# Neighbourhood attention: low parts of the keys padded to 128 rows, two heads together through transposes and value products, bias in one tile

## The chip, the cores and the metric

One Trainium2 chip, one of its cores. The metric is the device time of one execution in microseconds (us). TensorE (PE) multiplies, with its weight loads shown as PEld; VectorE (DVE), ScalarE (ACT) and GpSimd (POOL) do the rest, and SyncE (SP) issues most DMAs. "Line" L141 is line 141 of the kernel before.

## The reference

Two layers of a hybrid backbone over 512 latent tokens (an 8 x 64 grid) and 256 context tokens, 1024 features, all in float32. Layer 0 mixes by eight heads of two-dimensional neighbourhood attention (64 features each) beside four mLSTM heads; layer 1 by multi-head latent attention; each layer ends in a gated FFN with a depthwise convolution of width 3. The change touches the neighbourhood attention:

```python
def row_block(args):                 # one row of queries
    ...                              # bias: learned 2-D table in the 8 x 16 window, -1e30 outside
    s_lat = einsum('bqhd,bkhd->bhqk', q_row, k_band) * scale + bias
    s_ctx = einsum('bqhd,bkhd->bhqk', q_row, k_c) * scale
    p = softmax(concatenate([s_lat, s_ctx], axis=-1), axis=-1)
    nl = kh * GRID_W
    return einsum('bhqk,bkhd->bqhd', p[..., :nl], v_band) + einsum('bhqk,bkhd->bqhd', p[..., nl:], v_c)
```

A latent query thus reads its window and all context keys under one softmax. The context tokens attend to each other in the same eight heads (`dense_attention`, without a bias).

## The kernel before

The kernel is written with a tile framework: instructions are given in program order, tiles come from rings with a number of buffers, and a scheduler with its own estimate of durations then orders each engine's queue. Program order is priority; an instruction whose operands it expects late may be passed by later ones. Blocks under `tc.high_priority` (weight loads, `mix_split`) go ahead of their place. All semaphores come from the framework.

**Precision.** Most matmuls run in the one-pass float32r format. For accuracy an operand is split into `hi`, its rounded value, and `lo`, the rest, and a product is hi·hi + lo·hi + hi·lo, three matmuls into the same PSUM region (`proj`, `proj_steps`). The value products and transposes are plain float32; a float32 product leaves two records in the trace.

**Pairs of heads.** The eight heads go in four pairs, p_ = 0 to 3. `na_proj` computes queries, keys and values of a pair in 48 steps of three matmuls each: eight k tiles, 512 latent and 256 context columns, three projections (tiles `qp`, `kp`, `vp`). For head s of the pair, `qs[s]` holds the high part of the query in its own 64 rows and the low part in the other 64. `kd[s]` holds the high part of the key twice, in both halves of the rows. One 128-row matmul of `qs[s]` with `kd[s]` therefore gives hi·hi + lo·hi. The third product, hi·lo, is a 64-row matmul of the query's own half with `kl`, one tile that holds the low parts of both heads in its halves. `vtok` holds the values, tokens on the partitions: seven tiles of window columns and two of context.

**Attention of a pair** (`na_attn`). The 512 queries are four blocks j of 128 (8 rows x 16 columns), and each reads 256 latent keys (8 rows x 32 columns from column `KSTART[j]`) and 256 context keys.

- `scores(s)`, per j: four matmuls into a PSUM tile `sp`, kd and kl for the 256 latent columns, then kd and kl for the 256 context columns. One DVE instruction (L816) adds the bias, writes `P[j]` and takes the maximum; ACT takes the exponential, POOL divides by the sum. Then `fill(nf[0])` lets some projection steps of the next pair follow.
- `weighted(s, P)`: for each quarter `ks` of the 512 keys, four transposes into `ptp`, a copy to `pT` (ACT and DVE in turn), and products with `vtok` into `ops_`, 64 output rows per head: one of 512 columns for a context quarter, four of 128 for a latent one.
- `scores_c(s)`, `weighted_c(s, ...)`: the same for the context's own queries (`spc`, `Pc`, `ptc`, `pTc`, `opc`).

The order in a pair is scores of head 0, scores of head 1, `weighted` 0, `scores_c` 0, `weighted` 1, the output copy to `mix`, `scores_c` 1, `weighted_c` 0 and 1. `NF = (2, 3, 4, 6)` says how many projection steps follow a score block, a quarter's transposes, a context score and a context transpose; the last pair has `NF3 = (0, 1, 2, 3)` and, instead of a projection, 14 steps of the output projection (tile `yps`). The first pair is projected within the mLSTM stage.

**Bias.** Per head a DMA (L801) brings three kinds of 128 x 256 (left, inner, right blocks) from HBM into `bias_t[s]`, one of two tiles of 3 x 512 whose second halves are zero and belong to the context keys. The DMAs go through SP's queue, as do the weight loads (`wload`, L180).

**Elsewhere.** `ps_w` hands out three one-bank PSUM tiles in turn. `scratch` and the tag `sq` are small rings of `sqp`, two tiles each. `fcw` holds the FFN's convolution weights of both layers, loaded at the start. The gate rows of the mLSTM (`gps`, L581) are float32 products with weight tiles of 128 rows x 32 columns, k tile k in column group k mod 4 of the array.

Of the kernel before, what the change touches and what calls it, by code (L numbers as in the profile page):

```python
# [9 lines left out]
F32 = mybir.dt.float32  # L10
# [56 lines left out]
def hybrid_backbone_kernel(ctx: ExitStack, tc: tile.TileContext, *aps):  # L67
# [14 lines left out]
    def psum_open(**n):  # L82
        """n: tiles per tag; A tiles hold two banks, the others one"""
        if psum:
            psum["st"].close()
        st = ExitStack()
        psum["st"], psum["n"], psum["split"] = st, n, False
        psum["p"] = st.enter_context(tc.tile_pool(name="ps" + "".join(f"{k}{v}" for k, v in n.items()), bufs=1,
                                                  space=bass.MemoryType.PSUM, reuse_waits="tile"))
# [41 lines left out]
    fcw = cload("ffn_conv", [128, 2, 2 * NH, 4])  # L131
# [26 lines left out]
    def table(func, after):  # L158
        """has the activation table loaded ahead of its first use"""
        t = tiny.tile([128, 8], F32, tag="rv", name="tab")  # L160
        act(t[:, 0:1], after, func)
# [21 lines left out]
    def proj(o, w, x, cols, ks=tuple(range(KD)), first=True, last=True):  # L183
        """out[m, cols] = sum over k tiles of W[k, m]^T x[k, cols]; w units hold [k][128]."""
# [60 lines left out]
    def ada(l, part, get, pool, bufs):  # L245
        """modulation part (1024 columns) of layer l; column group j of the array takes 256 of them"""
# [19 lines left out]
    def ada_q(l, part, q, get, pool, bufs):  # L266
        """256 columns of a part; column group j of the array takes a quarter of the k tiles"""
# [59 lines left out]
    def mod_scale(l, part, norm, name, nv=2):  # L327
        """norm_g * (1 + scale)"""
# [14 lines left out]
    class Seg:  # L343
        """a run of tokens: width, offset in the padded layout, offset in the packed one, modulation column"""
# [30 lines left out]
    def step(n):  # L375
        """n steps of the norm chains in flight, oldest first"""
# [7 lines left out]
    def until(sg):  # L384
        """finish the chain of a run of tokens"""
# [3 lines left out]
    def sums4(ps, w, srcs, first, last):  # L389
        """column sums of four tiles, side by side in the array"""  # L390
# [4 lines left out]
    def sums_bc(ps, sg, name):  # L395
        """rstd on all partitions from the sums of sums4"""
# [7 lines left out]
    class YNorm:  # L404
        """sum of squares over the feature tiles of a branch output, then the gated residual"""
# [68 lines left out]
    # =============================== layer 0 ===============================  # L474
# [4 lines left out]
    with ExitStack() as l0:  # L479
# [38 lines left out]
        def x0_scale(q):  # L518
            """x * rstd * A for a quarter of the feature tiles"""
# [16 lines left out]
        def token_major(which, wus):  # L536
            """W[k, 512] with tokens on the output partitions; a k tile per step"""
# [39 lines left out]
        # gate rows, four feature tiles side by side in the array; the shift comes in with the bias  # L577
# [58 lines left out]
        # tri[:, 0]: k <= m ; tri[:, 1]: k >= m ; tri[:, 2]: row 127 ; tri[:, 3]: row 0  # L636
# [12 lines left out]
        # additive masks: msk[:, 0] allows column <= row, msk[:, 1] allows column >= row  # L649
# [9 lines left out]
        # running maxima of e along the scan, chunks and heads on partitions (the directions 32 apart)  # L659
# [52 lines left out]
        # -M in three exact pieces (rows 0, 32, 64 on), for its sums over the partitions to be rows of it  # L712
# [30 lines left out]
        def na_proj(p_, nq, res):  # L743
            """queries, keys and values of a pair of heads, in steps"""
# [19 lines left out]
            kl = nq.tile([128, T], F32R, tag="kl", name="kl")  # L764
            for s in range(2):
                r0, r1 = (0, 64) if s == 0 else (64, 128)
                act(kd[s][r0:r1, :], kp_[r0:r1, 0:T])
                tt(V, kl[r0:r1, :], kp_[r0:r1, 0:T], fr(kd[s][r0:r1, :]), ALU.subtract)
# [22 lines left out]
        def na_attn(p_, nw, bias_t, fill, qs, kd, kl, vtok):  # L791
# [6 lines left out]
            def scores(s):  # L798
                hd = 2 * p_ + s
                r0, r1 = rows[s]  # L800
                nc.sync.dma_start(out=bias_t[s][:, :, 0:256], in_=a["na_bias"][hd].rearrange("k p n -> p k n"))  # L801
# [5 lines left out]
                for j in range(4):  # L807
                    sp = ps_w("sp")
                    q_ = qs[s][:, j * 128:(j + 1) * 128]
                    qh_ = qs[s][r0:r1, j * 128:(j + 1) * 128]  # L810
                    lat = sp[:, 0:256].rearrange("p (f r c) -> p f r c", f=2, r=8)
                    mm(lat, q_, klat(kd[s], j), True, False)
                    mm(lat, qh_, klat(kl[r0:r1], j), False, True)
                    mm(sp[:, 256:512], q_, kd[s][:, TX:T], True, False)
                    mm(sp[:, 256:512], qh_, kl[r0:r1, TX:T], False, True)
                    V.tensor_tensor_reduce(out=P[j], in0=sp, in1=bias_t[s][:, BKIND[j], :],  # L816
# [9 lines left out]
            def weighted(s, P):  # L826
                r0, r1 = rows[s]
                for ks in (2, 3, 0, 1):
# [4 lines left out]
                    pT = nw.tile([128, 512], F32, tag="pT", name="pT", bufs=2)  # L833
                    if ks % 2:
# [3 lines left out]
                    if ks >= 2:  # L838
                        mm(ops_[r0:r1, 0:TX], vtok[:, 7 + ks - 2, r0:r1], pT, ks == 2, False)
                    else:  # L840
                        for j in range(4):
                            vi = VTILE[KSTART[j] + 16 * ks]
                            mm(ops_[r0:r1, j * 128:(j + 1) * 128], vtok[:, vi, r0:r1],
                               pT[:, j * 128:(j + 1) * 128], False, ks == 1 and j == 3)

            def scores_c(s):
                r0, r1 = rows[s]
                sp = ps_w("spc")
                for j in range(2):
                    q_ = qs[s][:, TX + j * 128:TX + (j + 1) * 128]  # L850
                    qh_ = qs[s][r0:r1, TX + j * 128:TX + (j + 1) * 128]
                    mm(sp[:, j * 256:(j + 1) * 256], q_, kd[s][:, TX:T], True, False)
                    mm(sp[:, j * 256:(j + 1) * 256], qh_, kl[r0:r1, TX:T], False, True)
# [5 lines left out]
                Pc = nw.tile([128, 512], F32, tag="P", name="Pc", bufs=8)  # L859
# [9 lines left out]
            def weighted_c(s, Pc, opc):  # L869
                r0, r1 = rows[s]  # L870
# [6 lines left out]
                pT = nw.tile([128, 512], F32, tag="pT", name="pTc", bufs=2)  # L877
                V.tensor_copy(out=pT, in_=pt)
                for kt in range(2):
                    mm(opc[r0:r1, 0:TC], vtok[:, 7 + kt, r0:r1], pT[:, kt * 256:(kt + 1) * 256],  # L880
                       kt == 0, kt == 1)
# [7 lines left out]
            weighted(0, P0)  # L889
            c0 = scores_c(0)  # L890
            weighted(1, P1)
            act(mix[:, p_, 0:TX].rearrange("p (r j c) -> p j r c", j=4, r=8),
                ops_.rearrange("p (j r c) -> p j r c", j=4, r=8))
            c1 = scores_c(1)
            opc = ps_x("opc")
            weighted_c(0, c0, opc)
            weighted_c(1, c1, opc)
            act(mix[:, p_, TX:T], opc[:, 0:TC])

# [1 line left out]
        if True:  # L901
# [4 lines left out]
            def ml_in(hd):  # L906
                qk = []
                for w_ in range(2):
# [9 lines left out]
                    # 2 silu(u) = (tanh(u / 2) + 1) u  # L918
# [16 lines left out]
            def ml_decay(hd, sT):  # L935
                """decay matrices times scores, both directions"""
                ws = []
                for d in range(2):
                    pump(MP[0][d])
                    # w^T[s, t]; fwd admits s <= t  # L940
# [108 lines left out]
        with ExitStack() as nas:  # L1049
# [3 lines left out]
            bias_t = [nb_.tile([128, 3, 512], F32, name=f"bias{i}") for i in range(2)]  # L1053
            for t_ in bias_t:
                act(t_[:, :, 256:512], zpad[:, 0, 0:1].unsqueeze(2).to_broadcast([128, 3, 256]))
# [10 lines left out]
            def wo_steps():  # L1066
                """the first output tiles but for the last pair of heads"""
# [28 lines left out]
        mix_split(3)  # L1096
# [592 lines left out]
```

## Time and profile before

| what | value |
|---|---|
| runs shown | 1888.87, 1886.98, 1885.5 us; median 1886.98 us |
| the profiled execution, first to last instruction (its only own time on record) | 1887.4 us |
| mean granted TensorE clock | 0.984 |
| PE busy | 97% of the span, 10546 matmul records |
| DVE, ACT, POOL busy | 62%, 40%, 14% |
| the stage of neighbourhood attention, 291.1 to 502.8 us | 211.7 us, PE busy 208.87 us |

Rows of the order of time read: start in us, length in us, engine, line, operation, output<-inputs, weight tile (rows*columns) and output form, number merged. Rows of groups read: line, engine, operation, output<-inputs, form, count | busy us, mean ns of one | idle time of the engine ahead of them and what ended it. Rows of waits read: the engine and what waited <- what it waited for: us in total, times, longest us. The ends of matmuls are modelled and neighbours overlap, so what a matmul costs is seen from one start to the next.

### The profile page before, as it was taken

Reading aid. Unit: us, or ns where it says so; the run is one execution under the profiler, and the core shown is the slowest. Engines: PE = TensorE matmul, PEld = TensorE weight load, DVE = VectorE, ACT = ScalarE, POOL = GpSimd, SP = SyncE. Lnnn points to the kernel's source line nnn. Section 1 sums busy time; section 2 is a strip of 40 time slices with the busy share of each in tenths; the row PEclk is TensorE's granted clock in tenths of the full one; section 3 lists DMA queues with packets and bytes.
Section 4 is the critical chain, followed back from the end, with each engine's and each line's share of the span. In section 5 each row is a group of like instructions: output and inputs, shape, how many; then the busy total and the mean of one; then the engine's idle time right before and its main releaser. Section 6 shows DMA issues by size and latency. Waiting matters only on the chain. (4 is left out here: it accounts for less than half of the span.)

```text
span 1887.4 us, 26712 instructions
## 1 busy us (share of the span) xinstructions
PE 1825.2 (97%) x10546; PEld 1492.1 (79%) x10546; DVE 1173.2 (62%) x2230; ACT 748.0 (40%) x1295; POOL 258.8 (14%) x312
## 2 busy tenths in 40 slices
PE   7999999999999999999999999899998999999997
PEld 4777787776678888888888887778887888888885
DVE  3383676345537676767666456888885574556655
ACT  3333454343334432222221334567784444334232
POOL 1000132122222000000000002444451100000000
PEclk8999999999999999999999999999999999999998
DMA  8343431112310333434432210100011213333221
GB/s 300 107 134 112 135 101 48 48 51 78 117 40 28 107 123 112 124 111 145 134 112 78 79 57 24 41 12 13 12 34 56 68 58 99 101 94 118 89 90 45
DMA packets 63196, 162.26 MB, mean 86 GB/s; under 512 B 6256, under 2 KB 19744, under 8 KB 63072
## 3 DMA queue, kind: packets, MB, share of 16 engines
q1 hardware_dynamic: 61616, 156.52, 26.4%
q0 software_dynamic: 1312, 3.91, 0.6%
q8 instruction: 83, 1.36, 0.3%
q14 instruction: 41, 0.34, 0.1%
q10 hardware_dynamic: 144, 0.13, 0.0%
HBM read 158.44 MB, written 2.10 MB: 85 GB/s over the span
## 5 line engine op out<-in xcount | busy, mean ns | idle before, releaser
L147 ACT ACTIVATE whi<-wraw 128x1024 fp32r<-128x1024 f32 x186 | 195.5, 1059 | 466.3 <-PE pu L141 220.0
L150 DVE TENSOR_TENSOR wlo<-wraw,whi 128x1024 fp32r<-128x1024 f32 x183 | 222.9, 1224 | 223.6 <-ACT whi L147 218.0
L141 PE MATMUL pu<-h,whi 128*128 128x258 f32 (+1 forms) x1280 | 318.6, 339 | 0.0
L141 PEld LDWEIGHTS pu<-h,whi 128*128 128x128 f32 x1280 | 219.7, 189 | 28.6 <-issue 0.8
L141 PE MATMUL pd<-hid,whi 128*128 128x512 f32 (+1 forms) x864 | 233.3, 358 | 1.5 <-DVE acc L150 1.5
L141 PE MATMUL pu<-h,wlo 128*128 128x512 f32 (+1 forms) x640 | 216.8, 339 | 0.0
L141 PEld LDWEIGHTS pd<-hid,whi 128*128 128x128 f32 x864 | 152.3, 188 | 28.4 <-DVE acc L150 3.1
L150 POOL TENSOR_TENSOR ry<-rv,mhalf 128x2 f32<-128x2 f32 (+2 forms) x26 | 23.8, 915 | 1013.9 <-DVE rv L153 1011.9
L141 PE MATMUL pd<-hid,wlo 128*128 128x512 f32 (+1 forms) x432 | 153.1, 356 | 0.0
L156 DVE SCALAR_TENSOR_TENSOR u<-pu,c_ffn_conv,u 128x769 f32<-128x769 f32 (+1 forms) x156 | 138.0, 885 | 21.6 <-ACT u L147 19.7
L150 DVE TENSOR_TENSOR acc<-pd,acc 128x512 f32<-128x512 f32 (+1 forms) x192 | 109.2, 586 | 48.6 <-PE pd L141 47.3
L141 PEld LDWEIGHTS pu<-h,wlo 128*128 128x128 f32 x640 | 121.0, 189 | 13.6
L141 PE MATMUL pu<-lb,whi 128*128 128x512 f32 x304 | 119.7, 394 | 0.0
L141 PE MATMUL pu<-hb,whi 128*128 128x512 f32 x304 | 119.0, 391 | 0.0
L141 PE MATMUL pu<-hb,wlo 128*128 128x512 f32 x304 | 118.3, 389 | 0.0
L156 DVE SCALAR_TENSOR_TENSOR av<-aw,s,av 128x512 f32<-128x512 f32 x140 | 102.4, 749 | 20.4 <-DMA aw<-in_ada_w_dram 19.9
L153 POOL TENSOR_SCALAR P<-P,rl 128x768 f32<-128x768 f32 (+1 forms) x96 | 85.6, 893 | 148.3 <-DVE nm L153 60.5
L141 PEld LDWEIGHTS pd<-hid,wlo 128*128 128x128 f32 x432 | 81.2, 189 | 11.7
L147 ACT ACTIVATE u<-pu,c_ffn_conv 128x770 f32<-128x770 f32 (+1 forms) x78 | 68.4, 877 | 39.5 <-PE pu L141 39.4
L141 PE MATMUL sp<-kr,qh 128*128 128x512 f32 (+1 forms) x256 | 72.6, 359 | 4.3 <-DVE kr L150 3.3
L141 PE MATMUL yps<-h,whi 128*128 128x512 f32 (+1 forms) x256 | 69.6, 360 | 0.0
L141 PEld LDWEIGHTS pu<-hb,whi 128*128 128x128 f32 x304 | 57.1, 188 | 13.2
(442 smaller groups left out, 3861.6 us busy)
## 6 DMA issues: line engine op xcount, KB each, us to landing
wraw<-in_ffn_up_dram SPq DMA_DIRECT2D x88, 512.0 KB, 3.6
aw<-in_ada_w_dram SPq DMA_DIRECT2D x112, 256.0 KB, 2.7
wraw<-in_ffn_down_dram SPq DMA_DIRECT2D x44, 512.0 KB, 3.6
aw<-in_ada_w_dram SPq DMA_DIRECT2D x40, 512.0 KB, 4.7
wraw<-in_w_in_dram SPq DMA_DIRECT2D x20, 512.0 KB, 3.6
wraw<-in_w_tok_dram SPq DMA_DIRECT2D x8, 512.0 KB, 4.2
wraw<-in_w_out_dram SPq DMA_DIRECT2D x8, 512.0 KB, 3.5
wraw<-in_w_o_dram SPq DMA_DIRECT2D x8, 512.0 KB, 3.5
```

The lines of the kernel that those rows point to most:

```text
L141: PE.matmul(out=o, lhsT=l, rhs=r, start=start, stop=stop)
L147: S.activation(out=o, in_=i, func=func, **kw)
L150: e.tensor_tensor(out=o, in0=x, in1=y, op=op)
L153: e.tensor_scalar(out=o, in0=x, scalar1=s1, scalar2=s2, op0=op0, op1=op1)
L156: V.scalar_tensor_tensor(out=o, in0=x, scalar=s, in1=y, op0=op0, op1=op1)
```

## The change

The low parts of the keys get a tile for each head, with zeros in the other head's rows, filled once for each of the two buffers (`kl_pair`); every score matmul then takes the whole `qs[s]`. Transposes and copies of a quarter are done for both heads (`turned`), and its products, the two heads in turn, follow one quarter later (`products`). The context's products alternate in the same way. `pT` has four buffers, the context probabilities move to the ring `sq`, and the bias of both heads lies in one tile of seven slices, three for each head and one of zeros. The convolution weights of layer 1 are loaded ahead of its FFN.

```diff
-    fcw = cload("ffn_conv", [128, 2, 2 * NH, 4])
+    fcw = [cload("ffn_conv", [128, 2 * NH, 4], a["ffn_conv"][:, 0])]
...
+        klz = {}
+        def kl_pair(nq):
+            if nq not in klz:
+                klz[nq] = [nq.tile([128, T], F32R, name=f"kl{s}") for s in range(2)]
+                for s in range(2):
+                    o = slice(64, 128) if s == 0 else slice(0, 64)
+                    ts(G, klz[nq][s][o, :], zpad[o, 0, 0:1].to_broadcast([64, T]), 1.0, 0.0, ALU.mult, ALU.add)
+            return klz[nq]
...
-            kl = nq.tile([128, T], F32R, tag="kl", name="kl")
+            kl = kl_pair(nq)
...
-                tt(V, kl[r0:r1, :], kp_[r0:r1, 0:T], fr(kd[s][r0:r1, :]), ALU.subtract)
+                tt(V, kl[s][r0:r1, :], kp_[r0:r1, 0:T], fr(kd[s][r0:r1, :]), ALU.subtract)
...
-                nc.sync.dma_start(out=bias_t[s][:, :, 0:256], in_=a["na_bias"][hd].rearrange("k p n -> p k n"))
+                nc.sync.dma_start(out=bias_t[:, 3 * s:3 * s + 3, :], in_=a["na_bias"][hd].rearrange("k p n -> p k n"))
...
-                    mm(lat, qh_, klat(kl[r0:r1], j), False, True)
+                    mm(lat, q_, klat(kl[s], j), False, True)
...
-                    mm(sp[:, 256:512], qh_, kl[r0:r1, TX:T], False, True)
-                    V.tensor_tensor_reduce(out=P[j], in0=sp, in1=bias_t[s][:, BKIND[j], :],
+                    mm(sp[:, 256:512], q_, kl[s][:, TX:T], False, True)
+                    bi = 3 * s + BKIND[j]
+                    V.tensor_tensor_reduce(out=P[j].rearrange("p (a b) -> p a b", a=2),
+                                           in0=sp.rearrange("p (a b) -> p a b", a=2), in1=bias_t[:, bi:7:6 - bi, :],
...
-            def weighted(s, P):
...
+            def turned(ks, Ps):
+                pts = []
+                for s, P in enumerate(Ps):
                     pt = ps_w("ptp")
                     for j in range(4):
                         tr(pt[:, j * 128:(j + 1) * 128], P[j][:, ks * 128:(ks + 1) * 128])
                     fill(nf[1])
+                    pT = nw.tile([128, 512], F32, tag="pT", name="pT", bufs=4)
+                    if s:
                         V.tensor_copy(out=pT, in_=pt)
                     else:
                         act(pT, pt)
+                    pts.append(pT)
+                return pts
+            def products(ks, pts):
+                if ks >= 2:
+                    for s, (r0, r1) in enumerate(rows):
+                        mm(ops_[r0:r1, 0:TX], vtok[:, 7 + ks - 2, r0:r1], pts[s], ks == 2, False)
+                    return
+                for j in range(4):
+                    vi = VTILE[KSTART[j] + 16 * ks]
+                    for s, (r0, r1) in enumerate(rows):
+                        mm(ops_[r0:r1, j * 128:(j + 1) * 128], vtok[:, vi, r0:r1],
+                           pts[s][:, j * 128:(j + 1) * 128], False, ks == 1 and j == 3)
...
-                Pc = nw.tile([128, 512], F32, tag="P", name="Pc", bufs=8)
+                Pc = sqp.tile([128, 512], F32, tag="sq", name="Pc")
...
-            weighted(0, P0)
-            c0 = scores_c(0)
-            weighted(1, P1)
+            cs = [scores_c(0)]
+            late = None
+            for ks in (2, 3, 0, 1):
+                pts = turned(ks, (P0, P1))
+                if late:
+                    products(*late)
+                late = (ks, pts)
+                if ks == 3:
+                    cs.append(scores_c(1))
+            ptc = [turned_c(0, cs[0])]
+            products(*late)
...
-            c1 = scores_c(1)
+            ptc.append(turned_c(1, cs[1]))
             opc = ps_x("opc")
-            weighted_c(0, c0, opc)
-            weighted_c(1, c1, opc)
+            for kt in range(2):
+                for s, (r0, r1) in enumerate(rows):
+                    mm(opc[r0:r1, 0:TC], vtok[:, 7 + kt, r0:r1], ptc[s][:, kt * 256:(kt + 1) * 256],
+                       kt == 0, kt == 1)
...
-            bias_t = [nb_.tile([128, 3, 512], F32, name=f"bias{i}") for i in range(2)]
-            for t_ in bias_t:
-                act(t_[:, :, 256:512], zpad[:, 0, 0:1].unsqueeze(2).to_broadcast([128, 3, 256]))
+            bias_t = nb_.tile([128, 7, 256], F32, name="bias")
+            act(bias_t[:, 6, :], zpad[:, 0, 0:1].to_broadcast([128, 256]))
...
+    fcw.append(accp.tile([128, 2 * NH, 4], F32, name="fcw1"))
+    nc.gpsimd.dma_start(out=fcw[1], in_=a["ffn_conv"][:, 1])
```

More of the change, by code (lines that the diff above doesn't have):

```diff
@@ L809, in scores @@
                     q_ = qs[s][:, j * 128:(j + 1) * 128]
-                    qh_ = qs[s][r0:r1, j * 128:(j + 1) * 128]
                     lat = sp[:, 0:256].rearrange("p (f r c) -> p f r c", f=2, r=8)
                     mm(lat, q_, klat(kd[s], j), True, False)
-                    mm(lat, qh_, klat(kl[r0:r1], j), False, True)
+                    mm(lat, q_, klat(kl[s], j), False, True)
                     mm(sp[:, 256:512], q_, kd[s][:, TX:T], True, False)
-                    mm(sp[:, 256:512], qh_, kl[r0:r1, TX:T], False, True)
-                    V.tensor_tensor_reduce(out=P[j], in0=sp, in1=bias_t[s][:, BKIND[j], :],
+                    mm(sp[:, 256:512], q_, kl[s][:, TX:T], False, True)
+                    bi = 3 * s + BKIND[j]
+                    V.tensor_tensor_reduce(out=P[j].rearrange("p (a b) -> p a b", a=2),
+                                           in0=sp.rearrange("p (a b) -> p a b", a=2), in1=bias_t[:, bi:7:6 - bi, :],
                                            scale=1.0, scalar=-3e38, op0=ALU.add, op1=ALU.max,
@@ L824, in scores @@
                 return P
-            def weighted(s, P):
-                r0, r1 = rows[s]
-                for ks in (2, 3, 0, 1):
+            def turned(ks, Ps):
+                pts = []
+                for s, P in enumerate(Ps):
                     pt = ps_w("ptp")
@@ L832, in weighted @@
                     fill(nf[1])
-                    pT = nw.tile([128, 512], F32, tag="pT", name="pT", bufs=2)
-                    if ks % 2:
+                    pT = nw.tile([128, 512], F32, tag="pT", name="pT", bufs=4)
+                    if s:
                         V.tensor_copy(out=pT, in_=pt)
@@ L837, in weighted @@
                         act(pT, pt)
[L838 to L844, printed above, removed]
+                    pts.append(pT)
[10 more added lines that the diff above has]
+                           pts[s][:, j * 128:(j + 1) * 128], False, ks == 1 and j == 3)
             def scores_c(s):
@@ L850, in scores_c @@
                     q_ = qs[s][:, TX + j * 128:TX + (j + 1) * 128]
-                    qh_ = qs[s][r0:r1, TX + j * 128:TX + (j + 1) * 128]
                     mm(sp[:, j * 256:(j + 1) * 256], q_, kd[s][:, TX:T], True, False)
-                    mm(sp[:, j * 256:(j + 1) * 256], qh_, kl[r0:r1, TX:T], False, True)
+                    mm(sp[:, j * 256:(j + 1) * 256], q_, kl[s][:, TX:T], False, True)
                 mxc = tiny.tile([128, 2], F32, tag="mxc", name="mxc")
@@ L867, in scores_c, with turned_c @@
                 return Pc
-            def weighted_c(s, Pc, opc):
-                r0, r1 = rows[s]
+            def turned_c(s, Pc):
                 pt = ps_w("ptc")
@@ L876, in weighted_c @@
                 fill(nf[3])
[L877 to L881, printed above, removed]
+                pT = nw.tile([128, 512], F32, tag="pT", name="pTc", bufs=4)
+                if s:
+                    V.tensor_copy(out=pT, in_=pt)
+                else:
+                    act(pT, pt)
+                return pT
             P0 = scores(0)
@@ L1161, in up_post @@
                     u = fw.tile([128, pw], F32, tag=f"u{g}", name=f"u{g}")[:, c0:c0 + w]
-                    cw = fcw[:, l, g * NH + j, :]
+                    cw = fcw[l][:, g * NH + j, :]
                     act(u, pu, AF.Identity, scale=cw[:, 1:2], bias=cw[:, 3:4])
```

## The prediction

> **What bounds the kernel now.** I read the page, then the table of stretches cut at the pairs of heads (each stretch runs from the first score matmul of one pair to that of the next), then who waited for whom on TensorE there, then the order of time inside a pair.
>
> ```profile
> span 1887.4 us, 26712 instructions
> PE 1825.2 (97%) x10546; PEld 1492.1 (79%) x10546; DVE 1173.2 (62%) x2230; ACT 748.0 (40%) x1295; POOL 258.8 (14%) x312
> ```
>
> ```profile
> 291.10:341.30 50.20, 50.13 (x260) 36.16 (x259) 24.45 (x79) 19.96 (x47) 14.09 (x21) 1.00 0.13 38
> 341.30:396.60 55.30, 55.26 (x281) 39.38 (x281) 23.16 (x55) 19.51 (x43) 9.89 (x16) 1.00 0.14 43
> 396.60:455.70 59.10, 57.45 (x294) 40.77 (x295) 33.05 (x72) 21.73 (x46) 17.45 (x29) 1.00 0.13 41
> 455.70:502.80 47.10, 46.03 (x185) 29.03 (x184) 26.51 (x66) 13.27 (x32) 12.62 (x17) 0.86 0.34 107
> ```
>
> The columns are the stretch, its length, then busy time (and count) of PE, weight loads, DVE, ACT and POOL, the granted clock, the DMA share and GB/s. The four pairs take 211.7 us, a ninth of the span, and TensorE is busy in all but 2.8 us of it; DVE, the next engine, has at most 33 of 59 us. TensorE waits little:
>
> ```profile
> PE vtp L144 <- ACT vt L147: 1.1, 1, 1.1
> PE ptc L144 <- POOL Pc L153: 1.1, 1, 1.1
> PE opc L141 <- DVE pTc L878: 0.5, 1, 0.5
> ```
>
> So the stage is as long as TensorE's instruction stream, and the question is what each matmul costs from its start to the next start. "Busy" hides that, since neighbouring records overlap. In the order of time:
>
> ```profile
> 307.37 0.28 PE L141 MATMUL sp<-kd,qs 128*128 128x256 f32 x1
> 307.58 0.39 PE L141 MATMUL sp<-kl,qs 64*128 64x256 f32 x1
> 307.89 0.39 PE L141 MATMUL sp<-kd,qs 128*128 128x256 f32 x1
> ...
> 309.46 0.38 PE L141 MATMUL sp<-kl,qs 64*128 64x256 f32 x1
> 309.77 0.49 PE L141 MATMUL kp<-h,whi 128*128 128x512 f32 x1
> ...
> 320.27 0.40 PE L141 MATMUL kp<-h,whi 128*128 128x256 f32 x2
> 320.50 0.28 PE L141 MATMUL kp<-h,wlo 128*128 128x256 f32 x1
> 320.72 1.09 PE L141 MATMUL ops<-pT,vtok 128*64 128x128 f32 x8
> ```
>
> A 256-column matmul of the projection follows its like after 0.12 us (two between 320.27 and 320.50). A score matmul of the same 256 columns takes 0.313 us: seven of them fill 307.58 to 309.77. They alternate between a weight tile of 128 rows (kd) and one of 64 rows (kl); a kd that follows a 128-row matmul of the projection starts without delay, and the first 64-row one comes 0.21 us later. So each change of the row shape costs about 0.19 us, about one load of weights that nothing covers. Repeated accumulation into one PSUM region is not the cause, as the projection does that too at 0.12.
>
> **The change, part by part.**
>
> *Low parts of the keys padded to 128 rows.* All score matmuls then use the same full q tile. No matmul is removed.
>
> ```profile
> L141 PE MATMUL sp<-kl,qs 64*128 64x256 f32 x64 | 25.4, 399 | 0.0
> L141 PE MATMUL sp<-kd,qs 128*128 128x256 f32 x64 | 22.9, 361 | 0.1
> L141 PE MATMUL ops<-pT,vtok 128*64 128x128 f32 x128 | 17.4, 279 | 0.0
> L141 PE MATMUL ops<-pT,vtok 128*64 128x512 f32 x32 | 16.9, 616 | 0.1
> L141 PE MATMUL opc<-pTc,vtok 128*64 128x256 f32 x32 | 8.6, 392 | 0.5 <-DVE pTc L878 0.5
> L141 PE MATMUL spc<-kl,qs 64*128 64x256 f32 x16 | 6.1, 381 | 0.0
> ```
>
> The latent scores are 32 blocks of four matmuls (x64 and x64). A block now costs 0.21 + 3 x 0.313 = 1.15 us and then 4 x 0.12 = 0.48: 0.67 saved, 21.4 in all. The context scores are 8 blocks (x16 and as many kd), taken at 0.313 each: 1.25 to 0.48, 6.2 in all. That the strided reads or the zero rows stream more slowly than the projection is not excluded: the kd already is a full 128-row read of the same view, and 307.37 to 307.58 bounds it at 0.21. With 0.21 the saving would be 160 x 0.10 = 16. I take 0.12, since the kd group alone after a like matmul is the nearest and holds its drain as well. Term: **-28**.
>
> *Two heads together in the value products.*
>
> ```profile
> 311.62 1.07 PE L141 MATMUL ops<-pT,vtok 128*64 128x512 f32 x2
> 312.62 0.50 PE L141 MATMUL kp<-h,whi 128*128 128x512 f32 x1
> ...
> 343.47 1.08 PE L141 MATMUL opc<-pTc,vtok 128*64 128x256 f32 x4
> 344.48 0.44 PE L144 MATMUL vtp<-c_ident,vt 128*128 128x128 f32 x2
> ```
>
> A float32 matmul leaves two records. A group of products, two records of 512, four of 256 or eight of 128 columns, takes 1.00 us until the next instruction may start, and a gap of about 0.10 stands ahead of it (320.50 + 0.12 to 320.72). There are 32 groups for the latents and 8 for the context (x128/8 + x32/2, x32/4), one head each: 40 x 1.10 = 44 us. A head's 64 columns are half of the array, head 0 the left half and head 1 the right one, and the new order puts them next to each other. Before, they never stood so with both operands ready, so the trace shows no pair of 64. It does show four quarters:
>
> ```profile
> 85.45 2.83 PE L581 MATMUL gps<-mix,wg 128*32 128x512 f32 x32
> 88.06 0.64 PE L141 MATMUL gps<-mod,wg 128*32 128x2 f32 x16
> ```
>
> These 32 records (16 of 512 and 16 of 256 columns, float32 as well, k tile k in column group k mod 4) took 2.61 us. At the pace of the products, one after the other, they would be 8 x 1.00 + 4 x 1.00 = 12: four ran at a time. So I take full overlap of two: 20 groups of both heads at 1.10 = 22, **-22**. The other end is no overlap: then a group of both heads costs 0.10 + 2 x 0.93, and -5 is left for the fewer changes of shape.
>
> The Trainium skill speaks against this: "TensorE: Matmul & The Clock Gate", Part 3 "The mechanism", says that a load of weights overlaps a running matmul only where the row groups differ, and that matmuls start in strict order. Both heads use all 128 rows, so by that rule the term would be near the -5. The gate matmuls above also use all rows, and they overlapped four at a time; here the trace differs, and I go by the trace.
>
> *What the new order moves.* Transposes (128 of them) and copies are as many as before. Each step now transposes a quarter of the keys for both heads, copies head 0's on ACT and head 1's on DVE, and runs the products of the step before. Four of the eight context copies go from DVE to ACT, at about the price of the others there; neither engine is near its limit. pT has four buffers for two. The context probabilities leave the ring of eight P tiles for two scratch tiles, but now all eight P tiles stay in use until the last transposes of the pair, so the next pair's first score can't be written sooner. What covers that is the tail of the pair: products, context transposes and copies, next pair's value transposes, its successor's query projection.
>
> Against the cover stands the fill: a pair projects 48 steps for the next one, and the code hands out 16 in the scores, 24 in the transposes and 8 in the context scores, which is all 48 by the last transpose. Before, the numbers were similar (60 asked for 48), and the stalls that it left are the three waits above, 2.7 us in all. I bound the new stalls by 0 and by that 2.7 at each of four pair ends, 10.8, and take the middle: **+5**. Where they come, the wait to be late next is the chain from a score to a transposed tile (DVE bias and maximum, ACT exponential, POOL division, ACT or DVE copy).
>
> *Bias in one tile, through a two-slice view (the bias, then a shared zero slice).*
>
> ```profile
> L816 DVE CUSTOM_DVE_ANT_0 P<-sp,bias 128x512 f32<-128x512 f32 x8 | 5.5, 692 | 7.4 <-PE sp L141 7.4
> L857 DVE TENSOR_REDUCE mxc<-spc 128x2 f32<-128x512 f32 x2 | 1.4, 691 | 5.3 <-PE spc L141 5.3
> DMA to landing us min/median/max: 3.1/3.3/5.0
> ```
>
> The reduction of the context already reads 512 elements as 2 x 256 and takes the same 0.69 us, so the view costs 0. The DMA per head carries the same bytes. One thing may change: the view spans from its slice to the last one, and if the second head's slices count as part of what the first head reads, their DMA waits on SP's queue for the first head's four reductions, with the weight loads of the next pair queued behind it, and the second head's first reduction waits for a landing of 3.3 us. Bounds 0 and 4 x 3.3 = 13; TensorE would have projection steps meanwhile, so I count 0 and leave it to the range. Two zero fills of 128x768 on ACT become one of 128x256, ahead of the stage where ACT has time: 0.
>
> *Zero halves and conv weights.* Four POOL instructions of 64x768, once for each of two buffers:
>
> ```profile
> L153 POOL TENSOR_SCALAR qs<-qx 64x512 fp32r<-64x512 f32 x2 | 1.2, 616 | 1.5 <-ACT qx L147 1.4
> ```
>
> So about 0.9 each, 3.7 us on an engine with 14 of 50 us busy, two in the stage before and two in pair 0; if a score had to wait for them, 3.7 at most. The two kl tiles get the same DVE subtractions as the one before. The FFN's conv weights of layer 1 come by a POOL DMA of their own, an issue of one instruction ahead of the second output projection, whose readers come tens of us later: 0.
>
> **Sum**: 1887.4 - 28 - 22 + 5 = 1842 against the span of the profiled execution, which is 0.4 us above the median of the three runs (1886.98; what lies around the span is too little to show). I forecast **1842 us**.
>
> **The rivals.**
>
> A. *The heads' products don't overlap.* For it: no row with two halves. Against it: the gate matmuls. The second term is -5: 1887 - 28 - 5 + 5 = 1859. The rule quoted above is this rival.
>
> B. *The pair ends starve.* With 50 us less TensorE work the chain of the other engines shows: the ring of P tiles empties only at a pair's last transpose, and the fill is used up. For it: the last pair, with 14 steps of fill, ran at 47 us with 46 busy only by a half-speed clock and by shape changes that now go. Against it: DVE at 33 of 59 us is the highest load. Its price:
>
> ```profile
> L147 ACT ACTIVATE P<-P,nm 128x512 f32<-128x512 f32 x8 | 5.8, 720 | 11.2 <-DVE nm L153 11.2
> L147 ACT ACTIVATE pT<-ptp 128x512 f32<-128x512 f32 x4 | 2.4, 592 | 6.3 <-PE ptp L144 6.3
> ```
>
> From score to copied tile it takes 0.69 (DVE, above) + 0.72 (ACT) + about 0.7 for POOL's division of as many elements + 0.59 (ACT) = 2.7 and some small instructions, say 3; twice that at each pair end is 24 in place of the 5: 1861.
>
> C. *Slower: the clock.* In the last pair the granted clock was 0.86, so 0.14 x 47 = 6.6 us of full speed were missing, and no wait of TensorE there was longer than 1.1 us. If gaps in the thinner stream bring the half-speed clock for long stretches, each us of it loses half a us. The 45 us gained are used up at 90 us of half speed, over half of the shortened stage; from there the kernel is slower, about 1890 to 1900. Pairs 0 to 2, with fill, ran at 1.00 throughout, which speaks against it. The Trainium skill, "TensorE: Matmul & The Clock Gate", "Why this matters for your kernels", asks only that no idle gap be over some 3 us; the trace does not agree that this is enough, as the clock fell here with gaps of 1.1 at most.
>
> D. *The padding brings nothing*, because the 0.31 us belong to something else than the row shape, such as the strided view. The context scores read a plain view:
>
> ```profile
> 322.05 0.38 PE L141 MATMUL spc<-kl,qs 64*128 64x256 f32 x1
> 322.36 0.39 PE L141 MATMUL spc<-kd,qs 128*128 128x256 f32 x1
> ```
>
> They start 0.31 apart as well, so I hold it unlikely. Then 1887 - 22 + 5 = 1870.
>
> E. *More than forecast*: no new stalls, and the last pair loses its slow clock (-5): 1832.
>
> **How the numbers follow.** Forecast with its own range 1834 to 1852: 0.65. A 0.10, B 0.12, C 0.03, D 0.04, E 0.06. The range 1829 to 1863 takes in A, E and most of B and leaves out C, D and the tail of B. Within 0.2% (3.8 us, about what a measurement of this kernel tells from no change): only a mixture of A, B and D, 0.02. Slower: C, 0.03. Faster: the rest, 0.95.
>
> **What would show it.** Right: score matmuls 0.12 us apart in blocks of four, all 128*128; products of the two heads starting within some 0.02 us of each other, a group of both in about 1.1 us; pairs 0 to 2 at 40 to 44 us instead of 50 to 59, the last at some 35; the rest of the kernel as long as before; TensorE's waits in the stage 5 to 10 us. Wrong: a second head's product that starts 0.4 us or more after the first one's (A); waits of transposes or scores on POOL or DVE of several us at each pair end (B); a clock under 0.9 in several pairs (C); 0.3 us between score matmuls of one shape (D); the second head's first reduction waiting for its bias to land.

## The result, and the profile after

The changed kernel took 1838.88 us (median of four runs, 1836.99 to 1839.91) against 1887.34 us (1885.5 to 1888.87) for the kernel before: a ratio of 0.9745, with a 95% interval of 0.9731 to 0.9758, 48.5 us faster. Five further runs on another chip gave 1838.66 us and 0.9746 (0.9732 to 0.9759). The forecast was 1842 us, range 1829 to 1863.

The head of the page of the changed kernel, whose profiled execution took 1836.99 us, 2.0 us more than its span:

```profile
span 1835.0 us, 26724 instructions
PE 1771.3 (97%) x10546; PEld 1468.3 (80%) x10546; DVE 1171.7 (64%) x2226; ACT 749.7 (41%) x1298; POOL 266.3 (15%) x317
```

As many matmul records as before (10546), in 53.9 us less busy time of TensorE. Where the time went is read from the stretches ahead of, in and behind the stage, first of the kernel before, then of the changed one (stretch, length, busy time and count of PE, weight loads, DVE, ACT and POOL, granted clock, DMA share, GB/s):

```profile
0.00:291.10 291.10, 269.40 (x1767) 208.77 (x1767) 167.15 (x462) 112.18 (x209) 30.99 (x47) 0.97 0.45 147
291.10:502.80 211.70, 208.87 (x1017) 145.33 (x1016) 107.18 (x271) 74.48 (x166) 54.05 (x83) 0.97 0.18 55
502.80:1887.40 1384.60, 1346.94 (x7764) 1138.02 (x7763) 898.85 (x1499) 561.38 (x921) 173.78 (x182) 0.99 0.25 78
```

```profile
0.00:290.86 290.86, 269.86 (x1768) 209.22 (x1768) 167.15 (x462) 111.14 (x208) 32.66 (x49) 0.96 0.45 147
290.86:451.79 160.93, 156.54 (x1014) 124.29 (x1013) 105.28 (x266) 76.99 (x170) 59.45 (x85) 1.00 0.23 73
451.79:1835.00 1383.21, 1344.89 (x7767) 1134.79 (x7766) 899.30 (x1500) 561.56 (x921) 174.21 (x183) 0.99 0.25 78
```

The stage went from 211.70 to 160.93 us, and the rest moved by 1.6. The same table of the changed kernel, cut at the pairs:

```profile
290.86:336.26 45.40, 41.10 (x272) 33.39 (x272) 27.19 (x83) 22.39 (x51) 17.14 (x25) 1.00 0.17 51
336.26:379.29 43.03, 43.03 (x284) 35.18 (x283) 23.26 (x54) 20.16 (x44) 10.47 (x16) 1.00 0.18 54
379.29:422.24 42.95, 42.95 (x284) 35.20 (x283) 30.66 (x66) 20.29 (x44) 19.80 (x28) 1.00 0.17 51
422.24:451.79 29.55, 29.46 (x183) 20.52 (x181) 24.17 (x63) 14.16 (x34) 12.03 (x16) 1.00 0.48 163
```

TensorE is still busy throughout in three pairs of four, so its stream still sets the stage. The last pair is shorter by 17.5 us, most of all, and its clock is 1.00 instead of 0.86. What TensorE waited for in the stage of the changed kernel:

```profile
PE hTp L144 <- DVE mix L153: 2.1, 1, 2.1
PE spc L141 <- DVE mx L827: 1.1, 1, 1.1
PE sp L141 <- DVE mx L827: 0.7, 1, 0.7
PE ptp L144 <- POOL P L153: 0.5, 1, 0.5
```

4.4 us, all of it in pair 0 and none at a pair's end. The order of time inside a pair of the changed kernel:

```profile
306.08 0.29 PE L141 MATMUL sp<-kd,qs 128*128 128x256 f32 x1
306.20 0.28 PE L141 MATMUL sp<-kl,qs 128*128 128x256 f32 x1
306.32 0.28 PE L141 MATMUL sp<-kd,qs 128*128 128x256 f32 x1
...
318.39 1.08 PE L141 MATMUL ops<-pT,vtok 128*64 128x512 f32 x4
319.40 0.39 PE L141 MATMUL spc<-kd,qs 128*128 128x256 f32 x1
...
333.04 0.43 PE L141 MATMUL ops<-pT,vtok 128*64 128x128 f32 x2
333.40 0.98 PE L144 MATMUL vtp<-c_ident,vt 128*128 128x128 f32 x7
334.31 0.44 PE L141 MATMUL ops<-pT,vtok 128*64 128x128 f32 x4
334.68 0.44 PE L144 MATMUL vtp<-c_ident,vt 128*128 128x128 f32 x2
335.05 0.87 PE L141 MATMUL ops<-pT,vtok 128*64 128x128 f32 x10
...
336.68 0.65 PE L141 MATMUL opc<-pTc,vtok 128*64 128x256 f32 x2
337.69 1.08 PE L141 MATMUL opc<-pTc,vtok 128*64 128x256 f32 x6
```

Score matmuls stand 0.12 us apart and are all 128*128. A group of both heads (x4: two records each) takes 1.01 us, 318.39 to 319.40, which one head took before. But at the pair's end the groups are broken up: the last quarter's 16 records come as 2, 4 and 10 with value transposes of the next pair between them, the context's 8 as 2 and 6.

To size the steps I added up, for each output tile, the time from each TensorE record of the stage to the next one. The difference before to after, -50.8 us, splits into scores 49.1 to 21.2 (-28.0), products `ops` and `opc` 39.7 to 24.8 (-14.9), the transposes, `ptp` and `ptc`, 19.9 to 15.9 (-4.0; 2.1 of it are the waits on `vt` and on `Pc`, which are gone), the output projection `yps` in the last pair 16.2 to 11.8 (-4.4; 47 records to 44), and +0.5 for all else. Waits are contained in these sums.

### The profile page after: what moved, and what is told of

It reads as the page before. It is cut to its first block, busy times and chain, and to the rows that moved or that the text cites. A ratio compares the mean times of both kernels' runs of the same rounds, so it can differ in the third digit from the quotient of the medians.

```text
span 1835.0 us, 26724 instructions
## 1 busy us (share of the span) xinstructions
PE 1771.3 (97%) x10546; PEld 1468.3 (80%) x10546; DVE 1171.7 (64%) x2226; ACT 749.7 (41%) x1298; POOL 266.3 (15%) x317
## 4 chain that ended last, share of the span: by engine, by line
PE 84%; DVE 7%; POOL 2%; issue 2%; ACT 2%; DMA 1%; DVEq 0%; POOLq 0%; ACTq 0%
PE pu L141 29%; PE pd L141 13%; PE yps L141 4%; PE sp L141 4%; PE qkp L141 3%; PE puf L141 3%; PE pdl L141 3%; PE vtk L141 3%; PE qp L141 2%; PE vp L141 2%; PE pt L144 2%; PE kp L141 2%; PE ot L141 2%; PE ops L141 1%; PE ysum L392 1%
## 5 line engine op out<-in xcount | busy, mean ns | idle before, releaser
L156 DVE SCALAR_TENSOR_TENSOR u<-pu,c_ffn_conv,u 128x769 f32<-128x769 f32 x80 | 81.1, 1014 | 10.5 <-ACT u L147 9.8
L1480 DVE TENSOR_REDUCE mx<-sp 128x1 f32<-128x768 f32 x64 | 60.9, 951 | 11.6 <-PE sp L141 11.0
L141 PEld LDWEIGHTS pu<-hb,wlo 128*128 128x128 f32 x304 | 57.1, 188 | 13.4
L141 PEld LDWEIGHTS pu<-lb,whi 128*128 128x128 f32 x304 | 57.1, 188 | 12.7
```

The source lines that it names most:

```text
L141: PE.matmul(out=o, lhsT=l, rhs=r, start=start, stop=stop)
L156: V.scalar_tensor_tensor(out=o, in0=x, scalar=s, in1=y, op0=op0, op1=op1)
L1480: V.reduce_max(out=mx[:, j:j + 1], in_=sp[:, 0:T], axis=AX.X)
```

## The experiments

**Padding alone.** Theory: the two large parts are independent, and the row shape is the price of a score matmul. Rival D of the prediction: the padding brings nothing.

```diff
-            kl = nq.tile([128, T], F32R, tag="kl", name="kl")
+            kl = kl_pair(nq)
...
-                    mm(lat, qh_, klat(kl[r0:r1], j), False, True)
+                    mm(lat, q_, klat(kl[s], j), False, True)
```

The second bias and the products stay as before; the late load of layer 1's convolution weights comes along to make room.

> The kernel before with the padding alone: low parts of the keys in two zero-padded tiles, every score matmul on 128 rows; order, products and bias as before (the layer-1 conv weights are loaded later, to make room). Theory (each change of the weight tile's rows costs some 0.19 us): 160 score matmuls go from 0.31 to 0.12 us, 28 us less, perhaps some more where the last pair's slow clock goes: 1854 to 1860. Rival (the padding pays only with the new order, since the chain of the other engines or the products hold TensorE otherwise): 1875 or more. Rival (0.31 us belong to the strided view): 1887.

Measured: 1858.32 us, ratio 0.9846 (0.9829 to 0.9863). The scores took 21.0 us, as in the full change. The last pair of this kernel:

```profile
437.72:472.06 34.34, 33.20 (x185) 23.43 (x184) 26.42 (x66) 13.25 (x32) 12.39 (x17) 1.00 0.45 146
```

D is out. The slow clock of the last pair is gone here as well, without the pairing.

**Two heads together, and the bias tile, without padding.** The diff is the change's, less `kl_pair` and the full `qs[s]` in the low products.

> The changed kernel without the padding: 64-row matmuls with one low tile, two heads together, bias in one tile. Theory (two column halves overlap): products 15 to 22 us less, some new waits: 1865 to 1875, scores still 0.31 us apart. Rival (the gain of the order is a gain of waits and clock in the last pair, not of overlap): the products stay at 1.0 us a head and the time is above 1878 unless the last pair's clock rises.

Measured: 1869.44 us, 0.9903 (0.9882 to 0.9923). The -17.3 us of this kernel and the -28.4 of the one above add up to -45.7 of -48.5: two nearly independent parts. In the order of time of this kernel, a group of both heads takes 1.01 us, and the unpadded scores behind it still start 0.31 apart:

```profile
321.99 1.08 PE L141 MATMUL ops<-pT,vtok 128*64 128x512 f32 x4
323.00 0.39 PE L141 MATMUL spc<-kd,qs 128*128 128x256 f32 x1
323.32 0.38 PE L141 MATMUL spc<-kl,qs 64*128 64x256 f32 x1
323.63 0.39 PE L141 MATMUL spc<-kd,qs 128*128 128x256 f32 x1
```

Its last pair keeps a slow clock, with TensorE busy in every us of it:

```profile
441.28:484.94 43.66, 43.66 (x183) 26.74 (x181) 24.37 (x63) 14.39 (x34) 11.82 (x16) 0.80 0.33 111
```

**Row shapes half as often.** If the change of shape is the price and not the 64-row matmul, then the kernel before gains by order alone: kd, kl, kl, kd in place of kd, kl, kd, kl has half the changes.

```diff
-                    mm(sp[:, 256:512], q_, kd[s][:, TX:T], True, False)
-                    mm(sp[:, 256:512], qh_, kl[r0:r1, TX:T], False, True)
+                    mm(sp[:, 256:512], qh_, kl[r0:r1, TX:T], True, False)
+                    mm(sp[:, 256:512], q_, kd[s][:, TX:T], False, True)
```

> The kernel before with one swap: in a block of score matmuls the context columns take the 64-row matmul first, so that the block goes 128, 64, 64, 128 rows in place of 128, 64, 128, 64 (the context scores of the context's own queries are left). Theory (the change of rows costs, not the 64 rows): two changes of four fall away in 32 blocks, 32 x 2 x 0.19 = 12 us less: 1875. Rival (a 64-row matmul is slow itself, or the strided view is): 1887.

Measured: 1872.58 us, 0.9918 (0.9897 to 0.9939), 14 us for two exchanged lines, of which the row shapes made only a part (see below). Its order of time:

```profile
306.36 0.28 PE L141 MATMUL sp<-kd,qs 128*128 128x256 f32 x1
306.57 0.50 PE L141 MATMUL sp<-kl,qs 64*128 64x256 f32 x2
307.00 0.51 PE L141 MATMUL sp<-kd,qs 128*128 128x256 f32 x2
307.44 0.50 PE L141 MATMUL sp<-kl,qs 64*128 64x256 f32 x2
307.87 0.39 PE L141 MATMUL sp<-kd,qs 128*128 128x256 f32 x1
308.10 0.40 PE L141 MATMUL kp<-h,whi 128*128 128x512 f32 x1
```

Two neighbours of one shape take 0.43 us together, 0.22 + 0.21 from start to start, whichever shape it is; with one shape throughout, two take 0.24. So the price lies on the change, about 0.19 us, about half of it in the matmul ahead of the change and half in the one behind, and a 64-row matmul is no dearer than a full one in the same place. The Trainium skill, "TensorEngine Tiling (Array Packing)", section "Key Properties", says that switching the tiling mode drains TensorE; a cost of 0.19 us at each change fits that, though the drain itself is not seen in the trace. The latent scores fell from 39.4 to 28.2 us, and the last pair lost its slow clock here too:

```profile
448.39:486.67 38.28, 37.21 (x185) 24.38 (x184) 26.60 (x66) 13.27 (x32) 12.62 (x17) 1.00 0.39 131
```

That the time came near the expected 12 us less is therefore partly luck. The clock gave 4.1 us in `yps` (16.2 to 12.1, 47 records each) and about 2.5 in the last pair's scores. In the other three pairs, at full clock in both kernels, the latent scores went from about 9.2 to 7.0 us each.

**Heads' products apart.** The changed kernel with the same tiles and copies, but with each head's products behind its own transposes' turn, so that the two heads' latent products mostly stand apart. The context's products still alternate, and at each pair's end one run of eight records of a head follows eight of the other.

```diff
-                pts = turned(ks, (P0, P1))
-                if late:
-                    products(*late)
-                late = (ks, pts)
+                new = []
+                for s, P in enumerate((P0, P1)):
+                    new.append((ks, s, turned_one(ks, s, P)))
+                    if late:
+                        products_one(*late[s])
+                late = new
```

> The changed kernel, but the products of a quarter follow the transposes of their own head one quarter later, so that the two heads' products no longer stand next to each other; same instructions. Theory (overlap of the halves makes the gain): each group takes 1.0 us again and has its own change of shape, 15 to 20 us more: 1853 to 1859. Rival (the order with a quarter's delay makes it): 1837 to 1842.

Measured: 1852.09 us, 0.9809 (0.9791 to 0.9826), 1 us below the range of the theory and far above that of the rival. A head alone takes 1.01 us again:

```profile
317.50 1.07 PE L141 MATMUL ops<-pT,vtok 128*64 128x512 f32 x2
318.51 0.66 PE L144 MATMUL ptp<-c_ident,P 128*128 128x128 f32 x4
```

`ops` goes from 18.8 to 30.8 us, nearly the 31.9 of before. What the pairing gains comes from neighbourhood, not from the copies or the delay by one quarter.

**How far ahead do products start?** Here the changed kernel's latent groups have head 0's four blocks first and head 1's four behind them. If matmuls start in strict order, head 1 starts with head 0's last; if each half has its own queue, at once.

```diff
-                for j in range(4):
-                    vi = VTILE[KSTART[j] + 16 * ks]
-                    for s, (r0, r1) in enumerate(rows):
+                for s, (r0, r1) in enumerate(rows):
+                    for j in range(4):
+                        vi = VTILE[KSTART[j] + 16 * ks]
```

> The changed kernel with the latent products in two runs: head 0's four blocks, then head 1's four, in place of the heads in turn. Theory (each half of the columns works off its own matmuls, so head 1's start under head 0's): 1837 to 1842, all sixteen records of a whole group in about 1.0 us. Rival (matmuls start strictly in the order of the queue, as the Trainium skill's page on TensorE has it): head 1's first waits for head 0's last to start, 0.75 us more in each of 8 groups: 1844 to 1846.

Measured: 1841.79 us, 0.9759 (0.9746 to 0.9772). The time lies in the theory's range, but the group took 1.51 us, which is neither of the two:

```profile
332.55 1.58 PE L141 MATMUL ops<-pT,vtok 128*64 128x128 f32 x16
334.06 0.66 PE L144 MATMUL ptc<-c_ident,Pc 128*128 128x128 f32 x4
```

The starts of its 16 records, in ns, show two chains with steps of 109 (160 after a chain's first):

```
chain 1:   0  160  269  379  488  597  706  815
chain 2:                     494  654  764  873  982 1091 1200 1309
```

The trace doesn't name the half that a record uses; I read the chains from the steps, with the queue in program order. The second chain's first record is then the ninth of the queue. It started 6 ns after the fifth, while the sixth to eighth were still waiting: it passed three. So I formed a third theory, a look-ahead of three waiting records, and tried it with runs of two blocks per head (four records): then the fifth record, which passes three, should start with the first.

```diff
-                for j in range(4):
+                for j, s in ((0, 0), (1, 0), (0, 1), (1, 1), (2, 0), (3, 0), (2, 1), (3, 1)):
```

> The changed kernel with the latent products in runs of two blocks: two of head 0, two of head 1, and again. In runs of four, head 1's first record started only when the fifth of head 0's eight had, with three of head 0's still waiting: 1.51 us a group in place of 1.02. Theory (TensorE looks past a few waiting matmuls, here three): with four records to a run head 1's first starts at once and a whole group takes 1.02 to 1.1 us: 1837 to 1841. Rival (any run of one head delays the other by the run's length less one): head 1's first starts 0.3 us late, 1.3 us a group.

Measured: 1842.21 us, 0.9752 (0.9737 to 0.9767), somewhat above what was expected though the stage was 162.0 us, beside 161.25 in a second profile of the changed kernel. The group:

```profile
334.48 1.14 PE L141 MATMUL ops<-pT,vtok 128*64 128x128 f32 x16
335.56 0.65 PE L144 MATMUL ptc<-c_ident,Pc 128*128 128x128 f32 x4
```

1.08 us, with the second chain 13 ns behind the first. The look-ahead of three fits both, and also the kernel with the heads apart, whose one run of eight and eight records per pair takes 1.51 us as well. The Trainium skill, "TensorE: Matmul & The Clock Gate", Part 3 "The mechanism", has matmuls start in strict order; the ninth record that started ahead of the sixth disagrees.

**Keeping the groups whole.** If the pieces at the pair ends are what the products fell short by, a group that can't be broken up gives it back. Head 1's first matmul goes ahead (its copy ends last), and the others are queued directly behind it with raised priority.

```diff
+            def together(*fs):
+                with tc.high_priority(offset=HPRIO):
+                    first = fs[0](1, *rows[1])
+                    with tc.issue_after(getattr(first, "ins", first)):
+                        for n, f in enumerate(fs):
+                            for s in (0, 1):
+                                if n or not s:
+                                    f(s, *rows[s])
```

> The changed kernel with the products of a step kept together: head 1's first, the others queued behind it, and a step ahead of the next pair's value transposes in priority. In the changed kernel the last quarter's and the context's products are broken into pieces at each pair end and the last pair's first quarter runs one head at a time; product matmuls take 25 us from start to start where 20 whole groups of 1.01 would take 20. Theory (the missing part of the products' gain is lost there): 4 to 7 us less, 1832 to 1835. Rival (the pieces fill waits, so whole groups only wait longer for the copies): 1837 to 1841.

Measured: 1833.77 us, 0.9717 (0.9704 to 0.973), 4.9 us below the changed kernel on the same chip. The groups at the end of its first pair are whole:

```profile
331.78 1.09 PE L141 MATMUL ops<-pT,vtok 128*64 128x128 f32 x16
332.81 0.39 PE L141 MATMUL vp<-h,wlo 128*128 128x256 f32 x1
...
335.23 1.08 PE L141 MATMUL opc<-pTc,vtok 128*64 128x256 f32 x8
336.24 0.44 PE L144 MATMUL vtp<-c_ident,vt 128*128 128x128 f32 x2
```

`ops` fell from 18.8 to 16.1 us and `opc` from 6.0 to 3.8: 4.9 us together, as in the theory. That it equals the gain in time is chance: the spans of the two profiles on this chip differ by 3.4 us (1835.0 to 1831.6), and new waits for the copies `pT`, 1.7 us in all, came in, as the rival had it. Raised priority and whole groups were changed together; what each does alone was not tried.

**The wait in pair 0.** The kernel above, with the mLSTM's last output one block later, so that the 2.1 us wait on `mix` goes.

```diff
-LATE3 = 1
+LATE3 = 2
```

> As the kernel with the products kept together, and in the first pair the mLSTM's last output comes after the scores of head 1 instead of between the heads' scores. In the changed kernel TensorE waits 2.1 us for DVE ahead of these transposes and 1.1 ahead of the context score. Theory (waits of the thinner stream): 2 to 3 us less than the kernel with the products kept together. Rival (DVE is the limit in this pair, so the wait only moves): the same time as that one.

Measured: 1833.03 us, 0.9717 (0.9704 to 0.973). Pair 0 of its profile was shorter, 41.66 us for 44.06 (the first row is of the kernel with whole groups, the second of this one):

```profile
289.76:333.82 44.06, 40.89 (x263) 33.57 (x263) 25.07 (x81) 21.44 (x48) 17.14 (x25) 0.96 0.15 43
```

```profile
290.59:332.25 41.66, 39.43 (x264) 32.50 (x263) 25.72 (x81) 21.55 (x48) 15.50 (x25) 1.00 0.15 45
```

Only 0.9 us of that is idle time (3.17 to 2.23); the rest goes with the clock, 0.96 to 1.00. What TensorE waited for in that pair of this kernel:

```profile
PE hTp L144 <- DVE rl L833: 1.4, 2, 1.2
...
PE hTp L144 <- DVE mix L153: 0.3, 1, 0.3
```

The wait on `mix` fell from 2.1 to 0.3 us, and a new one of 1.4 on the row sums' reciprocal took its place. The time is 0.7 us less, within the spread of either kernel's runs (2 to 5 us): inconclusive.

**The bias in one tile, alone.**

```diff
-                    V.tensor_tensor_reduce(out=P[j], in0=sp, in1=bias_t[s][:, BKIND[j], :],
+                    bi = 3 * s + BKIND[j]
+                    V.tensor_tensor_reduce(out=P[j].rearrange("p (a b) -> p a b", a=2),
+                                           in0=sp.rearrange("p (a b) -> p a b", a=2), in1=bias_t[:, bi:7:6 - bi, :],
```

> The kernel before with the bias in one tile alone (one zero slice, the two-slice view). Theory: no effect, 1885 to 1889, each of the 32 reductions at 0.69 us. Rival (the view ties the second head's bias to the first head's reads): the second head's first reduction in a pair waits for a landing of 3.3 us, up to 13 us more in all.

Measured: 1889.39 us over eleven runs against 1887.55, ratio 1.0007 (0.9998 to 1.0016): no effect. Its reductions in the stage (ns min/median/max, then first and last start):

```profile
L817 DVE CUSTOM_DVE_ANT_1 P<-sp,bias x28: 658/692/693, 293.4 to 470.9; 128x512 f32<-128x512 f32 x28
```

0.692 us, as before (28 of the 32; the other four, under another name, have the same median). The clock of its last pair was 0.86, as in the kernel before, over the same 47.1 us.

**The changed kernel again**, beside the kernels of the look-ahead and of the whole groups.

> The changed kernel again, as the measure for the three others on this chip: 1839, within 1836 to 1842.

Measured: 1838.66 us, 0.9746, as told in the result.

## Why the prediction was right, point by point

| step | forecast, us | measured, us |
|---|---|---|
| score matmuls at 0.12 instead of 0.31 | -28 | -28.0, about 2.5 of it from the slow clock |
| two heads' products overlap, with the transposes | -22 | -18.9 (-14.9 and -4.0), 2.1 of it waits |
| new stalls | +5 | idle 2.8 to 4.4: +1.6 |
| slow clock of the last pair | 0 (rival E: -5) | about -6.9 (-4.4 in `yps`, -2.5 in the scores) |
| bias tile, zero fills, convolution weights | 0 | bias within -0.4 and +3.0; rest outside the stage -1.6 together |

*Scores.* Right in cause; the exact size is partly luck. About 2.5 of the 28.0 us belong to the slow clock (below). In return, the matmul directly behind a block of scores became cheaper as well, which the term didn't count: a 256-column `qp` matmul there took 0.22 us to the next start before and 0.12 after, some 3 us in all. Padding alone gave the same 21 us of scores, and the exchanged order showed that the price is the change of row shape.

*Products.* The mechanism was right: with the heads apart the kernel takes 12 to 13 us more (0.9809 against 0.9746 of the kernel before), and the records of the two heads start 6 to 9 ns apart. Rival A, no overlap, is out, and with it, for two column halves, the rule quoted for it. The term was mis-sized because it counted 20 whole groups; the scheduler put other work between the two heads at every pair's end. Without the 2.1 us of waits it brought 16.8 of its 22 us. With the groups whole the products are at 19.9 us and the transposes at 15.3, -24.4 against before or -22.3 without those waits, so the price of a group was good and its count was not.

*Stalls.* The +5 was put at pair ends. No wait stood there: rival B is out, and what came, 2.1 us on `mix`, is in pair 0. The term was too high by 3.4 us.

*The clock.* The sum left it out, and E named it. Before, the clock was 0.50 in one stretch of the last pair:

```profile
464.50:478.20 13.70, 13.70 (x30) 8.91 (x31) 6.74 (x24) 4.50 (x12) 6.14 (x8) 0.50 0.40 148
```

Half of that stretch, about 6.8 us, was lost. It lay in `yps` and in the scores. The latent scores took 9.1 to 9.3 us from start to start in each of the first three pairs and 11.7 in the last. The table of stretches for `sp` alone, pairs 2 and 3 of the kernel before (here busy time of PE, weight loads, DVE and ACT), shows the same difference:

```profile
396.60:455.70 59.10, 9.82 (x32) 5.95 (x33) 5.53 (x8) 0.00 (x0) 1.00 0.13 41
455.70:502.80 47.10, 12.38 (x32) 7.32 (x32) 5.45 (x8) 0.00 (x0) 0.86 0.34 107
```

Of the twelve profiles, the three with every score changing its row shape had such a long slow stretch in the last pair (before 0.86, bias alone 0.86, pairing alone 0.80), and the nine with half the changes or none had 1.00 there. Rival C as it was priced, long stretches of half clock, is out as well: none of the seven profiles with the padding and the new order has one in the stage. In small, its mechanism does appear. In seven profiles TensorE waits about 2.1 us ahead of `hTp` in pair 0, and in six of them the clock is 0.50 for 3.4 us, beginning at the end of that wait or up to 1.5 us behind it; each costs 1.7 us. The first profile of the changed kernel has the wait without the slow stretch, the second has both (its pair 0):

```profile
289.57:335.28 45.71, 42.54 (x273) 34.56 (x272) 27.18 (x83) 22.50 (x51) 17.13 (x25) 0.96 0.15 49
```

Of the five profiles with a shorter wait there or none, only pairing alone had such a stretch.

*The base.* "What lies around the span is too little to show" was an error: about 2.0 us lie around it (1836.99 against 1835.0), and the sum started from the span. Set span against span, the forecast of -45 stands against 1887.4 - 1835.0 = -52.4. The 7.4 between them: the 5 of stalls (the waits that came are inside the other sums), 6.9 of clock and 1.6 in the rest of the kernel were not forecast as gains, while 2.5 of the scores, 3.1 of the products and 0.5 elsewhere in the stage did not come. The median time lies 3.9 us above that span: 2.0 around it, and 1.9 because the profiled execution was the fastest of its four. So 1842 is some 3 us from the time, closer than its parts, which is luck.

What stays open: whether and how the alternating shapes themselves bring the long half clock, and why in the last pair alone. With pairing alone it came without any idle time of TensorE; more the runs don't show.

*What was to be seen.* Scores 0.12 apart and all 128*128, products nearly simultaneous, groups of about 1.1 us, pairs 1 and 2 at 43 us: as written. Pair 0 took 45.4 us instead of 44 at most, the last 29.6 instead of some 35, and the waits were 4.4 us instead of 5 to 10.

## What to carry to other kernels

Where matmuls of two row shapes alternate, read their cost from start to start: here each change cost 0.19 us; zero rows took the changes away, and an exchanged order halved them. Matmuls in different column halves run side by side only while they stand close in the queue, so look in the order of time whether the scheduler kept them together; keeping them together, with raised priority, was worth 4.9 us more, and that version (1833.8 us) beats both kernels. When a forecast comes out right, check its terms one by one, since errors of 2 to 7 us cancelled here.

## What the runs showed of the hardware that I had not expected

- As read from the steps between starts, a matmul in the free column half started ahead of three records of the other half that were still waiting (ninth record 494 ns after the first), and no further ahead: 1.51 us for runs of eight records per head, 1.08 for runs of four, 1.01 to 1.03 for strict alternation.
- The clock fell to 0.50 in a stretch without idle time of TensorE. In the kernel with pairing alone, whose last pair had 43.66 us of 43.66 busy, it was 0.80 on average; with half the changes of row shape it was 1.00 in the last pair.
- After a wait of TensorE of about 2.1 us, the clock was 0.50 for 3.4 us in six profiles of seven.
